# A planned hybrid decoder layer on one core: later assumed landings, dearer ScalarE operations, another table of places in the queues

## The chip, the core and the metric

The kernel runs on one core of a Trainium2 chip. The metric is the device time of one execution in microseconds; the time before is the median of three runs. The five engines are TensorE (PE; PEld is its loading of weights), VectorE (DVE), ScalarE (ACT), GpSimd (POOL) and SyncE (SP). Each takes its instructions from its own queue in the order in which they were issued. SyncE and GpSimd also issue the transfers (DMAs) that bring the weights from the chip's memory.

## What is computed

One layer of a decoder trunk on x of 512 x 1024, in float32. One normed input goes through one combined projection into three groups of heads; a projection merges them; a dense SwiGLU network (width 2816) follows; both halves are residual.

```python
h = rmsnorm(x, norm_mix); mem_h = rmsnorm(mem, norm_mem)
proj = h @ w_in                                  # 1024 -> c_q, c_kv, k_rope, hq, hf, hi, hg, mq
y_mla = mla_group(...)                           # 4 heads, low-rank q and kv, rotary part, causal softmax
y_hg  = hgrn2_group(...)                         # 4 heads, gated linear recurrence in chunks of 64
y_mem = mem_group(mq, mem_h, w_mem_kv, ...)      # 4 heads, softmax over 256 memory tokens
x = x + concat(norm(y_mla), y_hg, norm(y_mem)) @ w_out
h2 = rmsnorm(x, norm_ffn)
x = x + (silu(h2 @ w_gate) * (h2 @ w_up)) @ w_down
```

The kernel reads w_in as `in_we`, `in_wf` and others, x transposed as `in_xT`, w_out as `in_wo`, w_gate, w_up and w_down as `in_wg`, `in_wu` and `in_wd`.

## The kernel before

**Precision.** Each float32 operand of a matmul is split into a rounded high part and the rest. `split` (L527) casts the high part on ScalarE (`A.copy`, or an activation with a scale) and subtracts it on VectorE. A product then takes three matmuls (`mm3`, L557): high by high, high by low, low by high. Tiles `xh`, `xl`, `wh`, `wl`, and `wr` in halves, hold such parts. A weight tile therefore passes through a transfer, a cast and a subtraction before TensorE can use it.

**Stages.** The program starts with the combined projection: tiles of x (`tm`, scaled by the gains in `p`) and of the weights (`p`, `tc`, then `wr`) are split, and the sum of squares of x is formed beside it (`td` <- `tm`). It goes on with the three groups of heads, the merging projection, and the feed-forward network from about 345 us on.

**Feed-forward network.** Its products are made in blocks of columns (512, 512, 384 of one half of the width, each with its partner in the other half). Within a block `seven` forms a two-by-two block product with seven products in place of eight. It loads weight tiles of 128 x 512 (128 x 384 in the last block) through SyncE's queue into the tags `mx`, `y` and at the start `xl`, and forms sums of weight blocks in place: GpSimd issues a transfer that adds a further block to the tile in the chip's on-core memory. This is `more(i, j)`:

```python
G.dma_start(out=e[k], in_=block(k, i, j), accum_op=ALU.add)
```

So a tile such as `mx_1099` is loaded, split and used, added to, split and used, and so on: an addition can be issued once the last split of the old contents has read the tile, and the next split waits for its landing. There are 105 such added transfers, 24 into `mx` from `in_wg`, 24 from `in_wu` and 33 from `in_wd` of 256 KB each, and 24 of 192 KB. `part` splits a tile with class 0 (`rec.first(0)`), that is, ahead of all other work. `prod` multiplies into two accumulator banks, `mm` and `at`.

**What sets the order.** No engine's order is written by hand. Class `Recorder` records every operation with the tiles it reads and writes. `run` (L266) then plans them: it walks through the operations with an assumed time for each, keeps for each engine the time at which it is free, and takes at each step the operation that can start first; among those that can start on the engine when it is free, the one of lowest `prio`, which is its number in the recording, plus 1,000,000 times its class, plus what the table `NUDGE` (L264) adds to it: a triple (a, b, d) adds d to operations a to b. Some operations may run on another engine (`alts`, from `others`): a copy, a square or a scaling on ScalarE or VectorE, say; the planner takes the engine that ends first, with 775 ns added for the move of one from ScalarE. A tile's buffer must have come free before an operation can write it. A transfer is assumed to land a time after its issue (L377 to L381), one transfer after another at 156 bytes per ns for GpSimd's and 320 for SyncE's. The times are `price` and `whole` (L186 and L204) and the table `LAT` between engines. `issue` (L404) then emits all instructions in the order planned; nothing of the planner is left at run time, where engines wait for each other by semaphores. In the profile all instructions carry the line at which `issue` emits them: L421 for groups of small matmuls, L424 for the rest. They are told apart by their tiles.

Names in the order below are tag, a number of the planner's that is the same in both programs, and a last number that is not.

Of the kernel before, what the change touches and what calls it, by code (L numbers as in the profile page):

```python
# [13 lines left out]
AF = mybir.ActivationFunctionType  # L14
# [33 lines left out]
class Recorder:  # L48
# [155 lines left out]
    def whole(self, o, ins, outs, n, m, fast):  # L204
        if o.eng == "scalar":
            fn = o.args[2] if o.name == "activation" else None
            if fn is not None:
                o.table = self.TABLES.get(str(fn).split(".")[-1])
            return (92 if fast else 45) + 0.835 * m + 90 * (fn == AF.Identity) + (190 if "accum_out" in o.kw else 0) + (100 if hasattr(o.kw.get("scale"), "ap") else 0)
        if o.eng == "vector":  # L210
            if o.name == "reciprocal":
                return 70 + 6.6 * m
            if o.name == "tensor_copy":
                return 66 + (0.55 if fast else 1.045) * m
            if o.name == "tensor_scalar":
                return 66 + (0.62 if fast else 1.045) * m + 60 * any(hasattr(a, "ap") for a in o.args[2:])
            if o.name == "memset":
                return 60 + 0.5 * m
            if o.name == "scalar_tensor_tensor":
                return 68 + 1.15 * m + 35 * hasattr(o.args[2], "ap")  # L220
            if o.name == "copy_predicated":
                return 118 + 1.045 * m
            return 68 + 1.045 * m
        if o.name == "memset":
            return 40 + m * 0.8
        if o.name == "tensor_scalar":
            return 244 + 0.84 * m
        return 170 + 2.17 * m
# [32 lines left out]
    IDLE = (1500, 3400)  # L261


    NUDGE = ((2288, 2299, 387), (4374, 4382, -19), (4519, 4568, -844), (1296, 1302, -1004), (4402, 4409, -54), (157, 208, -367), (1352, 1371, -477), (5505, 5507, -189), (3475, 3494, -1244), (3004, 3012, 13), (1981, 1982, 11), (374, 387, 86), (5158, 5164, -409), (4936, 4949, -66), (2039, 2066, 109), (1766, 1791, 700), (5579, 5592, -127), (5092, 5093, 164), (5378, 5383, 4), (4927, 4949, 130), (3745, 3796, -698), (3888, 3900, -443), (2600, 2610, -213), (2695, 2738, 57), (4403, 4409, -124), (3203, 3246, 29), (4683, 4734, 658), (782, 796, 421), (5455, 5461, -180), (1150, 1155, -13), (1118, 1129, -322), (5054, 5083, 300), (1955, 1976, -875), (435, 466, -183), (3034, 3049, 360), (2480, 2485, 125), (1486, 1510, 506), (3927, 3974, 15), (838, 880, 51), (4246, 4299, -11), (4243, 4268, -128), (4968, 4980, 162), (4356, 4372, -422), (2864, 2887, -16), (4823, 4831, -197), (2659, 2715, -5), (3944, 3945, 418), (2504, 2557, 78), (3092, 3101, 181), (265, 314, 7), (1719, 1724, 487), (785, 801, 227), (5531, 5543, 142), (3807, 3827, 371), (2712, 2764, 109), (1167, 1186, -349), (1413, 1457, -103), (2088, 2135, -179), (2654, 2675, 567), (4407, 4430, -251), (4998, 5015, 558), (2506, 2520, 59), (4792, 4801, 623), (3418, 3421, 1704), (4492, 4534, 47), (1999, 2011, 180), (1032, 1053, 351), (2940, 2973, 43), (2342, 2370, -524), (4945, 4949, 65), (283, 341, -78), (3368, 3376, 203), (981, 1004, 166), (5390, 5434, -9), (2863, 2922, 12), (3124, 3131, 58), (5026, 5031, 41), (986, 1036, 31), (5393, 5404, -387), (1584, 1640, -228), (4625, 4645, -63), (5120, 5124, 159), (4517, 4523, -32), (4646, 4660, 136), (3540, 3543, 351), (1664, 1667, -44), (1604, 1616, 232), (4454, 4455, -205), (2319, 2327, -158), (3890, 3932, 286), (4837, 4850, -602), (2173, 2184, 400), (2196, 2213, 100), (3099, 3150, -67), (3010, 3012, -13), (1765, 1782, 46), (1613, 1637, -942), (3968, 4014, -315), (681, 687, 478), (2089, 2118, 151), (4473, 4480, -5), (4342, 4360, -239), (4300, 4329, -247), (4580, 4586, -302), (4623, 4627, -518), (5114, 5133, -411), (1030, 1054, -249), (3123, 3150, -402), (4224, 4258, 339), (528, 532, -414), (1005, 1041, 511), (3895, 3915, 10), (3561, 3603, -80), (3309, 3371, 49), (3754, 3786, -555), (1978, 1990, -17), (722, 754, 255), (4588, 4598, -203), (3993, 4049, -99), (1133, 1146, -551), (3666, 3728, -142), (4921, 4949, -47), (2431, 2433, 243), (1381, 1382, 977), (5605, 5621, -133), (5366, 5377, -640), (1769, 1831, -65), (4434, 4436, 39), (711, 721, -102), (2277, 2312, -350), (4851, 4855, -387), (5404, 5417, -692), (619, 658, -92), (5274, 5289, -151), (3283, 3285, 245), (4700, 4733, -106), (1372, 1391, -127), (3205, 3216, 98), (3835, 3885, -48), (4510, 4513, 144), (5137, 5140, 108), (110, 169, -223), (1668, 1687, -350), (1323, 1342, -428), (1225, 1243, 213), (3020, 3073, -71), (1272, 1300, 293), (2106, 2122, 136), (2236, 2251, 496), (4226, 4287, -111), (4435, 4447, 110), (1237, 1247, -668), (4605, 4618, -147), (3583, 3615, 261), (1206, 1213, 35), (3202, 3209, 61), (4758, 4786, -239), (4462, 4490, 199), (3887, 3915, 15), (4719, 4729, 252), (4733, 4737, 334), (4528, 4580, -30), (2956, 2971, 461), (3693, 3700, -341), (3132, 3151, -7), (5044, 5090, -97), (528, 551, 98), (4222, 4225, -222), (907, 912, 509), (2209, 2240, 451), (4626, 4627, -165), (1908, 1923, -343), (3028, 3053, 287), (1468, 1496, 673), (3599, 3600, 15), (3961, 3963, -457), (5287, 5300, -16), (4511, 4543, -69), (549, 555, 115), (2739, 2743, 61), (234, 295, 19), (5417, 5460, 8), (983, 1021, -500), (2347, 2377, 72), (2923, 2931, -919), (1874, 1889, -470), (3315, 3355, -484), (721, 727, 196), (1444, 1493, 148), (829, 865, 1745), (3054, 3071, 190), (5475, 5483, -404), (5095, 5099, -388), (3004, 3013, 415), (3664, 3670, 70), (3080, 3090, -171), (5127, 5145, -201), (1968, 1997, 371), (1114, 1130, 88), (1485, 1527, 198), (4377, 4381, -462), (141, 164, 263), (3731, 3773, -617), (2059, 2060, 229), (3693, 3698, -518), (1539, 1551, 340), (4957, 5007, -149), (2211, 2235, -51), (860, 875, -93), (2154, 2174, 223), (5474, 5475, -141), (2610, 2650, -713), (4428, 4454, -53), (4834, 4842, -60), (1340, 1393, -154), (3696, 3734, -656), (4488, 4511, -408), (2676, 2716, -630), (1052, 1088, 267), (3650, 3651, 83), (311, 342, -148), (4295, 4298, 594), (4901, 4920, 34), (2118, 2144, 5), (2126, 2131, 378), (1978, 1993, 11), (4816, 4823, -117), (1725, 1764, -585), (4522, 4526, 113), (2880, 2896, 116), (3914, 3941, 8), (4556, 4557, 12), (1640, 1641, 1213), (1723, 1773, 218), (2024, 2062, -69), (4399, 4450, 29), (2857, 2870, -13), (113, 148, 169), (3422, 3458, -61), (2075, 2117, 34), (3605, 3614, -179), (3892, 3894, 292), (2940, 2944, -54), (5053, 5070, -584), (3245, 3260, 210), (964, 974, -167), (5514, 5545, -299), (4180, 4181, 243), (5423, 5437, 5), (4459, 4463, 133), (4212, 4228, -356), (780, 812, -89), (1883, 1888, 312), (3692, 3698, 150), (2011, 2039, 83), (5028, 5051, -44), (5572, 5597, 275), (4962, 4969, 122), (4902, 4909, 38), (4597, 4644, 338), (1627, 1660, 172), (369, 372, 683), (5261, 5274, -2958), (1781, 1796, -643), (5037, 5087, -219), (5249, 5266, -610), (5101, 5127, -73), (3067, 3080, 161), (1800, 1821, 296), (2144, 2156, 109), (1941, 1951, -634), (4197, 4232, 470), (3166, 3232, -158), (1549, 1560, 558), (277, 290, 124), (5172, 5175, 30), (3437, 3461, 45), (430, 440, -159), (5468, 5474, -26), (582, 588, 807), (3112, 3130, -644))  # L264

    def run(self):  # L266
        ops = self.ops
# [21 lines left out]
        table, dma, done, out, port, cold = None, 0.0, 0, [], 0.0, 0.0  # L289
        busy = {e: 0.0 for e in engs}  # L290
        begun, count = -1e9, self.AHEAD
        while done < len(ops):
# [79 lines left out]
            end = t + cost  # L372
# [4 lines left out]
            if o.dma:  # L377
                ap = o.kw["out"]
                nb = self._free(ap) * ap.ap[0][1] * 4
                dma = max(dma, t + 1100) + nb / (156.0 if o.eng == "gpsimd" else 320.0)  # L380
                end = dma + (2600 if o.eng == "gpsimd" else 1700)  # L381
            for k in o.new:
                tag = self.tiles[k][0]
                slots[tag].remove(min(slots[tag]))
# [1270 lines left out]
```

## Time and profile before

| | us |
|---|---|
| three runs | 693.21, 690.7, 689.88; median 690.7 |
| the profiled execution, its own time | 686.31 |
| its span in the profile | 684.5 |
| TensorE busy (matmuls) | 675.5 |
| VectorE busy | 589.6 |
| ScalarE busy | 397.5 |
| GpSimd busy | 98.7 |
| moved by transfers | 95.16 MB, mean 139 GB/s |

The profile is of one execution. A matmul's record includes the time in which it overlaps the one behind it, so that busy time on TensorE leaves out a part of each short stop. The number in brackets at the end of a row of the timeline is how long the engine was idle before the instruction, and whose end released it. In a row of busy time by stage the numbers are start and end, length, and for each engine its busy time and the count of instructions, then TensorE's granted clock, the share of time in which the core's 16 DMA engines were busy, and the GB/s that they moved.

### The profile page before, as it was taken

To read this page: it belongs to the slowest core of one execution; us is meant where nothing else is said; L and a number is where in the kernel's file an instruction comes from. 1 tells how busy PE (TensorE), PEld (TensorE's weight loads), DVE (VectorE), ACT (ScalarE), POOL (GpSimd) and SP (SyncE) were. 2 spreads that over 40 slices of the span, in tenths; PEclk is the share of its full clock that TensorE was granted. 3 is DMA by queue.
4 is the path that set the end of the run, shared out by engine and by line. 5 is a ranking of instruction groups with operands and counts; after the bars stand their busy time and mean duration, and the time that the engine had idled before them with its cause. 6 is when DMAs were issued, how large, how long until landed. Compare 5 with 4: busy or idle time off the path is not lost.

```text
span 684.5 us, 12877 instructions
## 1 busy us (share of the span) xinstructions
PE 675.5 (99%) x4684; PEld 560.8 (82%) x4684; DVE 589.6 (86%) x1313; ACT 397.5 (58%) x784; POOL 98.7 (14%) x132
## 2 busy tenths in 40 slices
PE   9999999999999999999999999999999999999997
PEld 5889978888888788888878788878878898889985
DVE  7879889889888989886779889778986988997996
ACT  7674346566667585665868546355643555553652
POOL 1000000000000000000122232223323133323330
PEclk9999999999999999999999999999999999999999
DMA  8522321032233143214387796887887778879754
GB/s 295 179 58 87 98 67 36 32 126 74 92 109 128 61 139 125 78 60 161 103 182 156 195 203 157 177 221 168 173 214 138 165 179 197 179 168 191 155 84 150
DMA packets 47871, 95.16 MB, mean 139 GB/s; under 512 B 5440, under 2 KB 13504, under 8 KB 47808
## 3 DMA queue, kind: packets, MB, share of 16 engines
q1 hardware_dynamic: 32256, 67.85, 30.2%
q0 software_dynamic: 15120, 25.96, 24.2%
q8 instruction: 37, 0.61, 0.4%
q10 hardware_dynamic: 432, 0.53, 0.2%
q14 instruction: 26, 0.21, 0.1%
HBM read 92.22 MB, written 2.10 MB: 138 GB/s over the span
## 4 chain that ended last, share of the span: by engine, by line
PE 73%; issue 13%; DMA 6%; POOL 4%; DVE 2%; ACT 1%; POOLq 0%; ACTq 0%; DVEq 0%
PE mm L424 45%; PE at L424 20%; PE tr L424 5%; POOL mx L424 4%; DMA mx<-in_wg 2%; DMA mx<-in_wu 2%; PE at L421 1%; DMA tc<-in_we 1%; DMA xl<-in_wg 1%; PE tr L421 1%; ACT wh L424 1%; DVE hd L424 0%; DVE tm L424 0%; DVE wl L424 0%; ACT hd L424 0%
## 5 line engine op out<-in xcount | busy, mean ns | idle before, releaser
L424 ACT CAST wh<-wr 128x512 fp32r<-128x512 f32 (+2 forms) x73 | 42.9, 597 | 46.6 <-PE mm L424 34.3
L424 ACT CAST wr<-mx 128x512 fp32r<-128x512 f32 (+1 forms) x77 | 45.6, 598 | 39.9 <-PE at L424 18.9
L424 DVE TENSOR_TENSOR wr<-mx,wr 128x512 fp32r<-128x512 f32 (+1 forms) x94 | 60.8, 658 | 5.7 <-ACT wr L424 5.0
L424 ACT CAST wh<-mx 128x512 fp32r<-128x512 f32 (+1 forms) x71 | 41.9, 598 | 38.0 <-PE at L424 25.8
L424 PE MATMUL mm<-xh,wh 128*128 128x512 f32 x152 | 59.8, 396 | 0.4 <-ACT wh L424 0.4
L424 PE MATMUL mm<-xl,wh 128*128 128x512 f32 x152 | 59.7, 395 | 0.0
L424 PE MATMUL mm<-xh,wl 128*128 128x512 f32 x152 | 59.5, 397 | 0.0
L424 DVE TENSOR_TENSOR wl<-wr,wh 128x512 fp32r<-128x512 f32 (+2 forms) x88 | 57.1, 659 | 2.8 <-PE mm L424 1.4
L424 DVE TENSOR_TENSOR wl<-mx,wh 128x512 fp32r<-128x512 f32 (+1 forms) x81 | 52.4, 659 | 4.7 <-PE at L424 1.9
L424 POOL DMA_DIRECT2D mx<-in_wg x36 | 31.4, 921 | 127.5 <-DVE wl L424 57.6
L424 PE MATMUL mm<-wh,xh 128*128 128x512 f32 (+2 forms) x136 | 47.3, 372 | 0.4 <-ACT wh L424 0.2
L424 PE MATMUL mm<-wh,hd 128*128 128x512 f32 (+2 forms) x140 | 44.4, 366 | 0.8 <-ACT wh L424 0.7
L424 POOL DMA_DIRECT2D mx<-in_wu x36 | 31.6, 917 | 86.4 <-DVE wl L424 42.6
L424 PE MATMUL mm<-wh,mx 128*128 128x512 f32 x128 | 44.0, 403 | 0.0
L424 ACT CAST wh<-y 128x512 fp32r<-128x512 f32 (+1 forms) x50 | 29.1, 594 | 23.7 <-PE at L424 16.6
L424 DVE TENSOR_TENSOR wl<-y,wh 128x512 fp32r<-128x512 f32 (+1 forms) x52 | 33.1, 652 | 7.7 <-PE at L424 2.7
L424 POOL DMA_DIRECT2D mx<-in_wd x33 | 28.7, 924 | 74.9 <-DVE wl L424 42.6
L424 POOL MEMSET pb<- 128x128 f32 x15 | 2.8, 204 | 234.5 <-PE at L424 209.1
L424 PE MATMUL mm<-wl,xh 128*128 128x512 f32 (+2 forms) x92 | 33.2, 361 | 0.6 <-DVE wl L424 0.6
L424 PEld LDWEIGHTS mm<-xh,wh 128*128 128x128 f32 x152 | 28.5, 188 | 6.2 <-ACT wh L424 0.5
L424 PEld LDWEIGHTS mm<-xh,wl 128*128 128x128 f32 x152 | 28.7, 189 | 5.5 <-DVE wl L424 0.2
L424 PEld LDWEIGHTS mm<-xl,wh 128*128 128x128 f32 x152 | 28.6, 188 | 5.6
(459 smaller groups left out, 1941.4 us busy)
## 6 DMA issues: line engine op xcount, KB each, us to landing
wr<-in_wf SPq DMA_DIRECT2D x19, 512.0 KB, 4.3
mx<-in_wd POOLq DMA_DIRECT2D x33, 256.0 KB, 5.0
wr<-in_wo SPq DMA_DIRECT2D x12, 512.0 KB, 3.8
mx<-in_wg POOLq DMA_DIRECT2D x24, 256.0 KB, 5.2
mx<-in_wu POOLq DMA_DIRECT2D x24, 256.0 KB, 5.0
mx<-in_wd SPq DMA_DIRECT2D x22, 256.0 KB, 4.1
y<-in_wd SPq DMA_DIRECT2D x22, 256.0 KB, 4.6
wr<-in_wt SPq DMA_DIRECT2D x8, 512.0 KB, 3.6
```

What stands on the lines that cost most here:

```text
L421: r = self.nc.tensor.matmul(get(a), lhsT=get(b), rhs=get(c), start=first, stop=last, skip_group_check=True)
L424: r = getattr(getattr(self.nc, o.eng), o.name)(*[get(a) for a in o.args], **{k: get(a) for k, a in o.kw.items()})
```

## The change

Three places of the planner change; no operation that is recorded does. ScalarE's assumed time of an operation rises by 8 ns where its inputs lie in on-core SBUF memory and by 11 ns otherwise. The assumed landing of each transfer is 0.8 us later on both queues. The table `NUDGE` is replaced: it had 281 triples and has 142, with other ranges and amounts.

```diff
--- before.py
+++ after.py
@@ -206,7 +206,7 @@
             fn = o.args[2] if o.name == "activation" else None
             if fn is not None:
                 o.table = self.TABLES.get(str(fn).split(".")[-1])
-            return (92 if fast else 45) + 0.835 * m + 90 * (fn == AF.Identity) + (190 if "accum_out" in o.kw else 0) + (100 if hasattr(o.kw.get("scale"), "ap") else 0)
+            return (100 if fast else 56) + 0.835 * m + 90 * (fn == AF.Identity) + (190 if "accum_out" in o.kw else 0) + (100 if hasattr(o.kw.get("scale"), "ap") else 0)
         if o.eng == "vector":
             if o.name == "reciprocal":
                 return 70 + 6.6 * m
@@ -261,7 +261,7 @@
     IDLE = (1500, 3400)
 
 
-    NUDGE = ((2288, 2299, 387), (4374, 4382, -19), (4519, 4568, -844), (1296, 1302, -1004), (4402, 4409, -54),
...
+    NUDGE = ((3247, 3249, 155), (4519, 4569, -1372), (295, 318, -135), (5018, 5033, 50), (640, 641, 177),
...
 
     def run(self):
         ops = self.ops
@@ -378,7 +378,7 @@
                 ap = o.kw["out"]
                 nb = self._free(ap) * ap.ap[0][1] * 4
                 dma = max(dma, t + 1100) + nb / (156.0 if o.eng == "gpsimd" else 320.0)
-                end = dma + (2600 if o.eng == "gpsimd" else 1700)
+                end = dma + (3400 if o.eng == "gpsimd" else 2500)
             for k in o.new:
                 tag = self.tiles[k][0]
                 slots[tag].remove(min(slots[tag]))
```

The instructions are the same in number and kind on TensorE and SyncE; a few operations change their engine: VectorE gets seven scalings of 128x128 more and ScalarE eight activations of that size fewer, GpSimd two more scalings, ScalarE six of VectorE's casts of 128x384, and the loads of function tables on ScalarE go from 12 to 10.

**The head.** On TensorE the first matmuls of the projection, into the accumulators `at_59` and `at_61`, from the second one after the warm-up on. `xh_17`, `xh_21`, `xh_25` are the high parts of the first three tiles of x, `wh_15`, `wh_19`, `wh_23` those of the first weight tiles. Before:

```order
L424 MATMUL at_59_1857<-xh_17_1845,wh_15_1837 128x512
L424 MATMUL at_61_1855<-xl_18_1853,wh_15_1837 128x512
L424 MATMUL at_61_1855<-xh_17_1845,wl_16_1843 128x512
L424 MATMUL at_61_1855<-xh_21_1860,wh_19_1849 128x512
L424 MATMUL at_59_1857<-xl_18_1853,wh_15_1837 128x512
L424 MATMUL at_59_1857<-xh_17_1845,wl_16_1843 128x512
L424 MATMUL at_59_1857<-xh_21_1860,wh_19_1849 128x512
L424 MATMUL at_61_1855<-xl_22_1869,wh_19_1849 128x512
L424 MATMUL at_61_1855<-xh_21_1860,wl_20_1862 128x512
L424 MATMUL at_59_1857<-xl_22_1869,wh_19_1849 128x512
L424 MATMUL at_59_1857<-xh_21_1860,wl_20_1862 128x512
L424 MATMUL at_61_1855<-xh_25_1881,wh_23_1875 128x512
```

and now:

```order
L424 MATMUL at_61_1861<-xh_17_1848,wh_15_1841 128x512
L424 MATMUL at_59_1855<-xl_18_1853,wh_15_1841 128x512
L424 MATMUL at_59_1855<-xh_17_1848,wl_16_1845 128x512
L424 MATMUL at_59_1855<-xh_21_1859,wh_19_1851 128x512
L424 MATMUL at_59_1855<-xl_22_1872,wh_19_1851 128x512
L424 MATMUL at_59_1855<-xh_21_1859,wl_20_1865 128x512
L424 MATMUL at_61_1861<-xl_18_1853,wh_15_1841 128x512
L424 MATMUL at_59_1855<-xh_25_1884,wh_23_1876 128x512
L424 MATMUL at_61_1861<-xh_17_1848,wl_16_1845 128x512
```

The accumulator of the other half now runs behind, and the first matmul with `xh_25` is the 9th, where it was the 13th. On ScalarE, the casts and squares that feed them (the first row is the high part of the second tile of x), before:

```order
L424 ACTIVATE xh_21_1860<-tm_5_1814,p_2_1801 128x512
L424 ACTIVATE td_41_1866<-tm_3_1805 128x512
L424 CAST wh_23_1875<-tc_6_1817 128x512
L424 ACTIVATE xh_25_1881<-tm_7_1819,p_2_1801 128x512
L424 ACTIVATE xh_27_1891<-tm_8_1823,p_2_1801 128x512
```

and now:

```order
L424 ACTIVATE xh_21_1859<-tm_5_1814,p_2_1801 128x512
L424 ACTIVATE td_41_1870<-tm_3_1805 128x512
L424 CAST wh_23_1876<-tc_6_1817 128x512
L424 ACTIVATE td_42_1879<-tm_5_1814 128x512
L424 ACTIVATE xh_25_1884<-tm_7_1819,p_2_1801 128x512
L424 ACTIVATE xh_27_1891<-tm_8_1823,p_2_1801 128x512
```

The square of `tm_5`, which VectorE did, now stands on ScalarE between `wh_23` and `xh_25`.

**A product of the first block.** On VectorE, from the split of `mx_1099` whose reading lets the second addition into that tile start (`wl_1135`), up to the split of the sum (`wl_1148`). `td` and the like are the sums of the seven products. Before:

```order
L424 TENSOR_TENSOR wl_1135_7337<-mx_1099_6824,wh_1134_7295 128x512
L424 TENSOR_TENSOR wl_1137_7344<-mx_1100_6868,wh_1136_7334 128x512
L424 TENSOR_TENSOR wl_1142_7351<-y_1112_7100,wh_1141_7341 128x512
L424 TENSOR_TENSOR td_1091_7329<-mm_1124_7227,td_1091_7329 128x512
L424 TENSOR_TENSOR wl_1144_7371<-y_1113_7116,wh_1143_7348 128x512
L424 TENSOR_TENSOR wl_1146_7381<-y_1114_7121,wh_1145_7374 128x512
L424 TENSOR_TENSOR wr_1140_7386<-y_1111_7056,wr_1140_7386 128x512
L424 CAST wh_1147_7402<-mx_1099_6824 128x512
L424 TENSOR_TENSOR wl_1148_7408<-mx_1099_6824,wh_1147_7402 128x512
```

and now:

```order
L424 TENSOR_TENSOR wl_1135_7310<-mx_1099_6841,wh_1134_7292 128x512
L424 CAST wr_1139_7319<-mx_1102_6900 128x512
L424 TENSOR_TENSOR wl_1137_7323<-mx_1100_6847,wh_1136_7314 128x512
L424 TENSOR_TENSOR wr_1139_7319<-mx_1102_6900,wr_1139_7319 128x512
L424 TENSOR_TENSOR wl_1142_7337<-y_1112_7063,wh_1141_7326 128x512
L424 TENSOR_TENSOR wr_1138_7334<-mx_1101_6858,wr_1138_7334 128x512
L424 TENSOR_TENSOR wl_1144_7350<-y_1113_7075,wh_1143_7341 128x512
L424 CAST wr_1140_7368<-y_1111_7055 128x512
L424 TENSOR_TENSOR wr_1140_7368<-y_1111_7055,wr_1140_7368 128x512
L424 COPY td_1091_7383<-mm_1115_7297 128x512
L424 TENSOR_TENSOR wl_1146_7388<-y_1114_7093,wh_1145_7353 128x512
L424 TENSOR_TENSOR td_1091_7383<-mm_1124_7223,td_1091_7383 128x512
```

The next row is the split `wl_1148`. The parts `wr_1139` and `wr_1138` are now formed between the two, and the cast `wh_1147` has gone to ScalarE.

**The last block of gate and up, and the first of down.** On ScalarE, from `wr_1418`, a part of the last gate and up block, on; `wh_1445`, `wh_1447` and `wh_1449` are the first of the down projection. Before:

```order
L424 CAST wr_1418_8667<-mx_1357_8020 128x384
L424 ACTIVATE tc_1350_8658<-tc_1350_8658,r2_996 128x384
L424 CAST wh_1419_8685<-mx_1358_8031 128x384
L424 CAST wh_1445_8694<-mx_1423_8326 128x512
L424 ACTIVATE tm_1353_8520<-tm_1353_8520,r2_996 128x384
L424 CAST wh_1447_8708<-mx_1424_8372 128x512
L424 CAST wh_1449_8716<-mx_1425_8415 128x512
```

and now:

```order
L424 CAST wr_1418_8678<-mx_1357_8050 128x384
L424 CAST wh_1445_8692<-mx_1423_8378 128x512
L424 CAST wh_1447_8698<-mx_1424_8391 128x512
L424 CAST wh_1449_8705<-mx_1425_8421 128x512
L424 ACTIVATE tm_1353_8531<-tm_1353_8531,r2_996 128x384
L424 CAST wh_1419_8718<-mx_1358_8059 128x384
```

The cast `wh_1419`, whose tile `mx_1358` is added to by GpSimd's transfer, moves behind the three. On SyncE's queue, the loads of the down projection, before:

```order
L424 DMA y_1435_8580<-in_wd 128x512
L424 DMA mx_1427_8632<-in_wd 128x512
L424 DMA y_1436_8649<-in_wd 128x512
L424 DMA y_1437_8665<-in_wd 128x512
L424 DMA y_1438_8672<-in_wd 128x512
L424 DMA mx_1428_8683<-in_wd 128x512
```

and now:

```order
L424 DMA y_1435_8607<-in_wd 128x512
L424 DMA y_1436_8624<-in_wd 128x512
L424 DMA y_1437_8630<-in_wd 128x512
L424 DMA y_1438_8652<-in_wd 128x512
L424 DMA mx_1427_8662<-in_wd 128x512
L424 DMA mx_1428_8676<-in_wd 128x512
```

The loads of `y_1436` to `y_1438` are issued ahead of that of `mx_1427`.

More of the change, by code (lines that the diff above doesn't have):

```diff
@@ new lines @@
+    NUDGE = ((3247, 3249, 155), (4519, 4569, -1372), (295, 318, -135), (5018, 5033, 50), (640, 641, 177), (3381, 3442, -139), (2895, 2918, 153), (5423, 5424, 172), (3587, 3615, 261), (974, 1004, 166), (5075, 5110, 35), (2910, 2917, -36), (5128, 5153, -187), (389, 428, 174), (4877, 4884, -76), (3986, 4047, -53), (2947, 3007, -50), (4331, 4335, 131), (4510, 4517, 223), (5158, 5160, -30), (4353, 4387, -36), (4374, 4386, -273), (731, 761, 65), (719, 754, 255), (829, 869, 2881), (4355, 4394, -55), (3926, 3927, 12), (4034, 4036, 154), (3711, 3770, 122), (883, 894, -55), (4051, 4052, -560), (388, 395, -95), (4947, 4949, 104), (510, 544, 266), (3163, 3166, 111), (5054, 5083, 546), (4682, 4744, 17), (4802, 4803, -8), (5092, 5093, 63), (5037, 5087, -195), (4170, 4198, -172), (5383, 5390, 57), (44, 56, -271), (1916, 1929, 48), (2975, 3002, 78), (5419, 5465, 23), (3004, 3013, 415), (967, 986, 393), (1167, 1186, -391), (3696, 3734, -656), (1968, 1987, 84), (5495, 5510, -44), (4346, 4395, 88), (5533, 5548, -719), (5474, 5488, 4), (714, 720, -70), (2018, 2022, -98), (4329, 4331, 96), (5141, 5142, 7), (970, 983, -537), (2949, 2972, 76), (1492, 1531, 40), (5048, 5088, -82), (5493, 5503, 195), (375, 380, 157), (5134, 5162, 62), (3793, 3825, -97), (3628, 3646, -103), (3044, 3059, 528), (4790, 4822, -70), (804, 808, 23), (1899, 1909, -158), (1005, 1044, 511), (1272, 1300, 802), (4287, 4308, 693), (4967, 4968, 277), (4597, 4601, 40), (4030, 4052, 24), (3440, 3483, 134), (5028, 5047, -57), (5261, 5274, -3656), (1781, 1796, -535), (3692, 3731, 109), (5158, 5161, -13), (3693, 3709, -191), (5515, 5545, -299), (5032, 5045, 66), (4931, 4994, 27), (4062, 4079, -4), (964, 974, -233), (983, 1021, -895), (4410, 4436, -251), (2665, 2706, 618), (5053, 5070, -584), (4705, 4708, 721), (3674, 3722, 79), (965, 974, -279), (4135, 4136, -10), (4443, 4502, 69), (4197, 4232, 470), (395, 447, -51), (4458, 4515, -104), (4719, 4736, 212), (4771, 4823, -497), (2209, 2240, 451), (4138, 4139, 447), (3745, 3796, -698), (3948, 4004, -75), (289, 301, 389), (4137, 4153, 164), (582, 588, 807), (4997, 5049, 35), (4479, 4502, -42), (3350, 3388, 18), (3303, 3304, 88), (5096, 5102, -20), (2619, 2641, 29), (4569, 4621, -35), (2132, 2164, -132), (3590, 3631, -26), (2878, 2901, 152), (3815, 3827, 1366), (5414, 5422, 132), (4973, 4976, 19), (358, 406, 736), (2944, 2972, 27), (5151, 5156, 490), (5117, 5123, 251), (4370, 4381, 41), (681, 693, 401), (2318, 2346, -33), (2816, 2817, 265), (2031, 2043, -234), (721, 727, 179), (4216, 4222, -628), (5114, 5133, -367), (5150, 5158, -212), (5578, 5603, 97), (1190, 1191, 13), (4483, 4524, -350), (754, 782, -83), (4459, 4515, 334))
```

1 line of the change is left out of this document (removed).

## The prediction

> **What bounds the kernel now.** I read the page's head and busy line first, then busy time by stage, then the chain of waits, and last the timeline of TensorE at each place where it stops. The page says:
>
> ```profile
> span 684.5 us, 12877 instructions
> PE 675.5 (99%) x4684; PEld 560.8 (82%) x4684; DVE 589.6 (86%) x1313; ACT 397.5 (58%) x784; POOL 98.7 (14%) x132
> PEclk9999999999999999999999999999999999999999
> ```
>
> TensorE is busy for 675.5 of 684.5 us at full granted clock, so all its idle time is 9.0 us. Its matmuls run at a fixed spacing: the chain holds twelve in a row without a wait, and these two transfers:
>
> ```profile
> 438.75 6.73 DMA mx<-in_wg
> ...
> 505.16 6.79 DMA mx<-in_wu
> ...
> 603.39 2.72 PE mm L424 x12
> ```
>
> 2.72/12 = 0.227 us for a matmul of 512 columns, three quarters of that (0.17) for 384. The orders of the two programs hold the same matmuls, so what can change is TensorE's stops. By stage (length, then busy time of PE, PEld, DVE, ACT and POOL, PE clock, share of the DMA engines, GB/s):
>
> ```profile
> 0.00:20.00 20.00, 18.46 (x67) 11.72 (x68) 15.06 (x26) 14.58 (x26) 2.39 (x9) 1.00 0.73 253
> ...
> 60.00:120.00 60.00, 59.43 (x1037) 51.51 (x1036) 53.40 (x155) 28.42 (x67) 0.00 (x0) 1.00 0.23 75
> 120.00:180.00 60.00, 59.95 (x621) 50.42 (x620) 54.96 (x157) 37.24 (x75) 1.48 (x8) 1.00 0.24 80
> 180.00:240.00 60.00, 59.68 (x304) 49.16 (x303) 52.30 (x138) 38.01 (x79) 0.77 (x4) 1.00 0.30 97
> 240.00:300.00 60.00, 59.90 (x472) 49.82 (x471) 52.25 (x149) 39.46 (x97) 2.40 (x6) 1.00 0.29 98
> 300.00:360.00 60.00, 59.85 (x343) 47.57 (x343) 45.73 (x103) 42.18 (x93) 6.20 (x7) 1.00 0.54 145
> 360.00:440.00 80.00, 79.93 (x365) 64.65 (x365) 72.63 (x128) 45.11 (x79) 21.35 (x25) 1.00 0.79 179
> 440.00:480.00 40.00, 39.26 (x171) 31.48 (x170) 31.18 (x53) 22.66 (x38) 9.69 (x12) 1.00 0.85 192
> 480.00:520.00 40.00, 39.31 (x171) 31.45 (x171) 35.58 (x60) 20.29 (x35) 10.89 (x14) 1.00 0.88 190
> ...
> 560.00:600.00 40.00, 39.19 (x200) 34.56 (x200) 36.20 (x66) 23.67 (x45) 11.97 (x14) 1.00 0.87 199
> ...
> 670.00:684.50 14.50, 10.51 (x45) 7.92 (x44) 8.69 (x17) 3.01 (x6) 0.00 (x0) 0.99 0.39 134
> ```
>
> Subtract PE from length. The first 20 us lose 1.54 and the last 14.5 lose 3.99, mostly start and drain. The attention and projection stages (60 to 360) lose 0.57 + 0.05 + 0.32 + 0.10 + 0.15 = 1.19. The feed-forward stages lose 0.07 + 0.74 + 0.69 + 0.81 = 2.31, all but 0.07 of it in those where the DMA engines are 0.85 to 0.88 busy. A matmul's record (about 0.39) is longer than its spacing (0.227), so busy time hides some 0.17 of each stop: a stop is therefore measured from start to start.
>
> **FFN landings: minus 3.0 us.** TensorE at the four worst places:
>
> ```profile
> 444.54 0.84 PE L424 MATMUL mm<-wr,v 128*128 128x512 f32 x3
> 446.05 0.50 PE L424 MATMUL mm<-wh,v 128*128 128x512 f32 x1 [0.67 <-DVE wh L424]
> ...
> 511.64 0.39 PE L424 MATMUL at<-wh,hd 128*128 128x512 f32 x1
> 512.72 0.50 PE L424 MATMUL mm<-wh,hd 128*128 128x512 f32 x1 [0.69 <-ACT wh L424]
> ...
> 574.32 0.34 PE L424 MATMUL at<-wh,pth 128*128 128x384 f32 x1
> 574.87 0.50 PE L424 MATMUL mm<-wh,xh 128*128 128x512 f32 x1 [0.21 <-ACT wh L424]
> 575.20 0.40 PE L424 MATMUL at<-wh,xh 128*128 128x512 f32 x1
> ...
> 575.96 0.33 PE L424 MATMUL mm<-wr,pth 128*128 128x384 f32 x1
> 576.89 0.50 PE L424 MATMUL mm<-wl,xh 128*128 128x512 f32 x1 [0.60 <-DVE wl L424]
> ```
>
> At 446.05 three matmuls from 444.54 should have been followed at 445.22: 0.83 late. At 512.72: 1.08 - 0.23 = 0.85. At 574.87: 0.55 - 0.17 = 0.38. At 576.89: 0.93 - 0.17 = 0.76. After a stop the second matmul starts 0.33 behind the first (574.87 to 575.20), not 0.227, so each costs 0.11 more. Sum: 0.83 + 0.85 + 0.38 + 0.76 + 4 x 0.11 = 3.26. I take 3.0, since a later stop of some tenths is likely to be left at one of them.
>
> The cause is a landing each time. The first two are the chain's transfers: added in place by a GpSimd DMA issued at 438.75 and 505.16, landed 6.73 and 6.79 later, where the medians are
>
> ```profile
> mx<-in_wg POOLq DMA_DIRECT2D x24, 256.0 KB, 5.2
> mx<-in_wu POOLq DMA_DIRECT2D x24, 256.0 KB, 5.0
> ```
>
> The other two are behind a waiting instruction:
>
> ```profile
> 573.78 1.03 ACT L424 CAST wh<-mx 128x384 fp32r<-128x384 f32 x2 [0.68 <-DMA mx<-in_wg]
> ...
> 575.54 0.69 DVE L424 TENSOR_TENSOR y<-y,y 128x512 f32<-128x512 f32 x1 [0.66 <-DMA y<-in_wd]
> ```
>
> ScalarE stood 0.68 for wh_1419's input with wh_1445 queued behind; VectorE stood 0.66 for y_1436 with wl_1446 queued behind.
>
> The planner assumes for 262,144 bytes on GpSimd's queue, if no other transfer is ahead, 1100 + 262144/156 + 2600 ns = 5.38 us: the median with a little room, but 1.4 less than the two late ones. Now it is 6.18. What that buys is counted in the order. Between the matmul that lets the second addition into mx_1099 start and the first that needs the sum stand 29 matmuls before (29 x 0.227 = 6.6 us, less than the 6.73 plus cast and split), and 37 now (8.4). For mx_1265 it is 30 (6.8) against 40 (9.1). ScalarE now has wh_1445, wh_1447 and wh_1449 ahead of wh_1419, and SyncE issues y_1436 ahead of mx_1427, which waits for a VectorE read. So all four stops go. Over all 105 added transfers, 13 leads were shorter than 32 matmuls (7.3 us), now 6; the shortest few (2 and 14 matmuls) stay. If those take the place of what went, the gain is 0; if the later small stops go too, 3.5.
>
> [...]
>
> **The program's head: plus 1.1 us.** Matmuls 13 and 14, 15, and 17 of the first projection, and ScalarE ahead of them:
>
> ```profile
> 9.36 0.73 PE L424 MATMUL at<-xh,wh 128*128 128x512 f32 x2
> 10.15 0.50 PE L424 MATMUL at<-xl,wh 128*128 128x512 f32 x1
> ...
> 10.72 0.40 PE L424 MATMUL at<-xh,wh 128*128 128x512 f32 x1
> ```
>
> ```profile
> 7.12 0.62 ACT L424 ACTIVATE td<-tm 128x512 f32<-128x512 f32 x1
> 8.06 0.63 ACT L424 CAST wh<-tc 128x512 fp32r<-128x512 f32 x1 [0.33 <-DMA tc<-in_we]
> 8.60 1.33 ACT L424 ACTIVATE xh<-tm,p 128x512 fp32r<-128x512 f32 x2
> ```
>
> The square td_42 moves from VectorE to ScalarE, between wh_23 (8.06) and xh_25 (8.60). ScalarE starts its next operation 0.54 after one of this size (8.06 to 8.60), so xh_25 starts near 9.13 in place of 8.60. Its first matmul came 0.76 after that start (9.36) and so comes at 9.89. It is also the 9th matmul in place of the 13th, so the four that used to fill the time stand behind it. The 17th then starts at 9.89 + 0.33 + 7 x 0.227 = 11.8 against 10.72: 1.1 later. The first ten loads are the same, so no transfer gives this back; if the later squares leave ScalarE freer, 0.8, and 1.3 if the next splits slip too.
>
> **The middle: 0.** In the stages from 60 to 360 the order changes in many rows, seven scalings of 128x128 move from ScalarE to VectorE, and two table loads go:
>
> ```profile
> L424 DVE TENSOR_SCALAR tm<-tm,rkn 128x128 f32<-128x128 f32 x4 | 1.0, 284 | 0.0
> ```
>
> ```profile
> L424 ACT ACT_TABLE_LOAD x12 | 15.4, 1283 | 2.3 <-issue 2.1
> ```
>
> 7 x 0.284 = 2.0 us more for VectorE, which is at most 55 of 60 busy there; 2 x 1.283 = 2.6 less for ScalarE, at most 42 of 60. Both lie beside matmuls, and TensorE's whole loss there is 1.19. A dense VectorE could turn the 2.0 into a wait, and the loads could have been what it waited for: minus 2 to plus 2, taken as 0, since the idle rows are nearest to it.
>
> **The tail: plus 0.1.** One of the last two accumulators is finished nine matmuls ahead of the other and the last operand comes some 0.2 later; the closing addition and the output transfer are the same.
>
> **The sum.** The profiled execution took 686.3 (span 684.5 and 1.8 around it). 686.3 - 3.0 + 1.1 + 0.0 + 0.1 = 684.5, so minus 1.8. The timed runs, 689.88 to 693.21, have their median 690.7, which is 4.4 above the profiled one: executions differ by more than the stops seen here. With one program at one clock, transfers that land later than in this trace are the candidate. If they are, longer leads take part of the 4.4; a quarter, 1.1, is my choice between none and all. 690.7 - 1.8 - 1.1 = 687.8.
>
> **The rivals.**
> *The excess goes too.* If all 4.4 us are late landings and the leads now cover them: 690.7 - 1.8 - 4.4 = 684.5. For it: at 0.85 to 0.88 busy engines, landings have a long tail (6.7 to 6.8 against 5.0 to 5.2). Against: some leads stay short, and the excess may lie in the start.
> *The leads buy nothing.* If landings are late because transfers queue on shared engines, issuing earlier only queues earlier, and the stops come back elsewhere. Only the head's 1.1 is left: 691.8. For it: the stops stand where the engines are busiest (0.85, 0.88, 0.87). Against: what the leads gain is eight to ten matmuls, 1.8 to 2.3 us, more than any of the stops.
> *Slower.* Earlier issue bunches the loads; at 440 to 520 the engines have an eighth left. If the old stops stay and three more transfers land as late as the first two (0.85 + 0.11 each), 3 x 0.96 = 2.9 is added beside the head: 690.7 + 1.1 + 2.9 = 694.7. It decides from a median landing above 6 us on GpSimd's queue. Against: bytes and bank reads are the same, and the queues' waits for reads bind them as before.
>
> **How the numbers follow.** Forecast 42%, excess gone 25%, leads worthless 18%, slower 15%. About 0.5%, 3.45 us, is what a measurement of this kernel can tell from no change: faster is below 687.2, slower above 694.2. The forecast's own range is 685.3 to 690.3 (middle plus or minus 2, quarter or half a us of the leads); it splits into 16% faster and 26% same. The second case gives 23 and 2, the third 15 same and 3 slower, the fourth 2 same and 13 slower. Together 39, 45 and 16%. The range runs from 683.0, below the second case by its unknown middle, to 694.0, which leaves out most of the slow case.
>
> **What would show it.** Right: no stop above 0.5 us at the four places, GpSimd's medians still 5.0 to 5.2, a TensorE idle sum in the feed-forward stages below 1 us, and the first xh-by-wh matmul of the third pair at about 9.9. Wrong: new stops above 0.5 behind other landings; medians above 6 us; more than 2 us of idle time from 60 to 360 with VectorE as releaser; or a profiled time near 684.5 with timed runs that keep their 4.4 or more.

## The result and the profile after

The changed kernel takes 684.23 us (median of 8 runs, 682.09 to 685.23) beside 688.45 for the kernel before (8 runs, 687.01 to 693.21): a ratio of 0.9925 over all runs, with a 95% interval of 0.9899 to 0.9951 (the two medians alone give 0.9939). A second measurement, told with the experiments, has 0.9944. By the medians of the two it is faster by 4.2 and 3.7 us. The forecast was a fall of 2.9 us, to 687.8.

The profiled execution took 682.81, 3.5 less than that of before:

```profile
span 681.0 us, 12877 instructions
PE 672.5 (99%) x4684; PEld 562.4 (83%) x4684; DVE 588.5 (86%) x1312; ACT 393.8 (58%) x781; POOL 100.3 (15%) x134
```

The same stages as before (start and end, length, busy time of PE, PEld, DVE, ACT and POOL, TensorE's granted clock, share of the DMA engines, GB/s):

```profile
0.00:20.00 20.00, 16.66 (x60) 10.50 (x61) 14.26 (x26) 14.58 (x26) 2.38 (x9) 1.00 0.74 253
...
60.00:120.00 60.00, 59.50 (x1037) 51.25 (x1037) 51.87 (x150) 28.18 (x65) 0.00 (x0) 1.00 0.24 75
120.00:180.00 60.00, 59.91 (x617) 50.39 (x616) 55.56 (x164) 34.70 (x70) 1.52 (x8) 1.00 0.25 80
...
440.00:480.00 40.00, 40.00 (x177) 32.34 (x176) 32.95 (x55) 23.08 (x38) 9.58 (x12) 1.00 0.88 198
480.00:520.00 40.00, 40.00 (x177) 32.69 (x176) 34.34 (x58) 20.77 (x36) 11.33 (x13) 1.00 0.84 181
...
560.00:600.00 40.00, 40.00 (x201) 35.75 (x200) 38.40 (x70) 22.92 (x44) 13.08 (x15) 1.00 0.88 191
```

TensorE is now busy all the time in the stages where it stood 0.74, 0.69 and 0.81 us, with the DMA engines as busy as before. The first 20 us lose 3.34 in place of 1.54. What went is seen in the waits for landings between 340 and 670 us. Each row gives engine, tile, the transfer waited for, total us, times and the longest. Before, ScalarE and VectorE:

```profile
ACT wh L424 <- DMA mx<-in_wu: 6.5, 5, 2.5
ACT wr L424 <- DMA mx<-in_wg: 4.8, 1, 4.8
ACT wh L424 <- DMA mx<-in_wg: 1.8, 3, 0.7
ACT wr L424 <- DMA mx<-in_wd: 1.6, 2, 1.3
ACT wr L424 <- DMA mx<-in_wu: 0.3, 1, 0.3
...
DVE y L424 <- DMA y<-in_wd: 1.4, 2, 0.8
DVE wh L424 <- DMA mx<-in_wg: 1.1, 1, 1.1
```

With four small rows of VectorE's more that is 20 us in 20 waits. In the changed kernel VectorE has none, and ScalarE these:

```profile
ACT wh L424 <- DMA mx<-in_wd: 3.2, 2, 2.5
ACT wh L424 <- DMA mx<-in_wu: 1.8, 2, 1.3
```

The transfers themselves land no sooner. GpSimd's added ones take 5.9 us at the median from in_wg, where they took 5.2:

```profile
mx<-in_wd POOLq DMA_DIRECT2D x33, 256.0 KB, 4.9
mx<-in_wg POOLq DMA_DIRECT2D x24, 256.0 KB, 5.9
mx<-in_wu POOLq DMA_DIRECT2D x24, 256.0 KB, 5.2
```

Counted in the traces, 10 of the 105 added transfers took over 6.5 us before, and 19 and 17 in the two profiles of the changed kernel. So the order gives the landings more time, and does not make them earlier.

For the account below, the time that TensorE loses in a stretch is summed from start to start: the distance between two matmuls, less the usual spacing of that shape (0.227 us for 512 columns). Unlike idle time this sees short stops in full. In us:

| stretch | before | changed | difference |
|---|---|---|---|
| first 20 us | 2.08 | 3.66 | +1.58 |
| 20 to 340 | 15.30 | 15.96 | +0.66 |
| from 340 | 8.44 | 2.74 | -5.70 |
| together | 25.82 | 22.36 | -3.46 |

### The profile page after: what moved, and what is told of

The parts are those of the page before. It is cut to its first block, busy times and chain, and to the rows that moved or that the text cites. A ratio compares the mean times of both kernels' runs of the same rounds, so it can differ in the third digit from the quotient of the medians.

```text
span 681.0 us, 12877 instructions
## 1 busy us (share of the span) xinstructions
PE 672.5 (99%) x4684; PEld 562.4 (83%) x4684; DVE 588.5 (86%) x1312; ACT 393.8 (58%) x781; POOL 100.3 (15%) x134
## 4 chain that ended last, share of the span: by engine, by line
PE 58%; DVE 4%; issue 0%; ACT 0%; DVEq 0%; ACTq 0%
PE mm L424 31%; PE at L424 24%; PE tr L424 3%; DVE tm L424 1%; DVE wl L424 1%; DVE xh L424 1%; DVE wr L424 0%; DVE tc L424 0%; DVE v L424 0%; DVE xl L424 0%; PE tr L421 0%; ACT wh L424 0%; DVE hd L424 0%; DVE pb L424 0%; DVE mvq L424 0%
## 5 line engine op out<-in xcount | busy, mean ns | idle before, releaser
L424 ACT CAST wh<-wr 128x512 fp32r<-128x512 f32 (+2 forms) x76 | 44.4, 595 | 43.5 <-PE mm L424 25.8
L424 ACT CAST wh<-mx 128x512 fp32r<-128x512 f32 (+1 forms) x75 | 43.7, 597 | 30.9 <-PE at L424 22.4
L424 PE MATMUL at<-wh,xh 128*128 128x512 f32 x88 | 31.9, 393 | 0.0
```

Of the source, the lines that this page charges most:

```text
L424: r = getattr(getattr(self.nc, o.eng), o.name)(*[get(a) for a in o.args], **{k: get(a) for k, a in o.kw.items()})
```

## The experiments

Seven of the twelve kernels run a written-out order: the planner's loop is replaced by two lists, and all that comes after it is unchanged.

```diff
     def run(self):
-        ops = self.ops
-        for a, b, d in self.NUDGE:
...
+        names = {"t": "tensor", "v": "vector", "s": "scalar", "g": "gpsimd", "y": "sync"}
+        out = []
+        for n, e in zip(ORDER, WHERE):
+            o = self.ops[n]
+            o.eng = names[e]
+            o.name, o.args, o.kw = o.alts[o.eng][:3]
+            out.append(o)
+        return out
```

ORDER holds the numbers of the operations and WHERE the engine of each, taken from the plan of before, from the changed plan, or from one up to a planned time and the other behind it; in two kernels some places are then moved by hand. Times are medians; the kernel before ran at 687.0 to 687.1 beside all of them.

### The changed kernel once more

Without an edit, beside 20 runs of the kernel before. 

> The changed kernel once more, beside the runs of before that the experiments share. Theory (its gain is the 3.5 us between the two traces, feed-forward network minus head and middle): 687.04 - 3.5 = 683.5, a ratio of 0.995. Rival (the first ratio of 0.9925 holds): 681.9.

Measured: 683.38 us (9 runs, 682.77 to 686.06) against 687.10, a ratio of 0.9944 (0.9921 to 0.9967): what the two traces give. The profiled execution of this measurement is one of the longer ones, 685.93; the last section tells why.

### Where the gain lies: the two plans joined

**The head of before, then the changed order** (joined at 20 us). 

> The first 20 us of the planned order are those of before, all that follows is in the changed order. Theory (the changed order of ScalarE and TensorE at the head costs 1.1 us): 1.1 below the changed kernel, 683.1, and TensorE loses 2.1 to 2.5 us in its first 20 us where the changed kernel lost 3.7. Rival (the first loads only landed later in that one execution, and the order at the head is harmless): 684.2, the same as the changed kernel, and a loss of 3.2 or more.

Measured: 682.95 us (0.9940, 0.9926 to 0.9954). The row of its first 20 us:

```profile
0.00:20.00 20.00, 18.32 (x64) 11.66 (x65) 14.50 (x25) 14.13 (x25) 2.39 (x9) 1.00 0.75 253
```

TensorE idles 1.68 there, near the 1.54 of before. Summed from start to start it loses 2.7, a little more than the 2.1 to 2.5 expected, and less than the rival's 3.2. So the order at the head does cost time. The median of 682.95 is only 0.4 below the 683.38 of the changed kernel's second measurement, and 1.0 below the median of all its 17 runs, 683.98.

**The order of before up to 340 us, then the changed one.** 

> The planned order of before up to 340 us, then that of the changed kernel. Theory (the whole gain lies in the feed-forward network, where the trace of before loses 8.4 us to stops and that of the changed kernel 2.7): 688.45 - 5.7 = 682.8, faster than the changed kernel by some 1.4. Rival (only the four stops of the prediction go, 3.3 us, and the rest is a difference between executions): 685.2. Second rival (the gain lies ahead of the feed-forward network or in both): above 687.

Measured: 683.59 (0.9952, 0.9939 to 0.9966), where 682.8 was expected of the theory. From 360 us on it is the changed kernel's picture, and one wait between 340 and 360 us, at the seam, takes 2.2 us:

```profile
360.00:660.00 300.00, 300.00 (x1440) 256.01 (x1439) 266.47 (x473) 168.18 (x306) 82.10 (x95) 1.00 0.81 179
```

```profile
PE mm L424 <- DVE hd L424: 2.2, 1, 2.2
```

That wait belongs to the joining: neither of the two kernels has it. The expected 682.8 was counted from 688.45; from the 687.10 beside this kernel the gain is 3.5, and with the seam's 2.2 it is the theory's 5.7. The time alone would suit the first rival's gain of 3.3 as well; what decides is that TensorE's stops between 360 and 660 us are gone.

**The changed order up to 340 us, then that of before.** 

> The planned order of the changed kernel up to 340 us, then that of before. Theory: 688.45 + 1.1 (head) + 0.7 (middle) = 690.2, with the late landings and TensorE's stops of before back in the feed-forward network. Rival (the early part brings some of the gain): 687 or less.

Measured: 692.26 (1.0077, 1.0063 to 1.0091). Here too the seam costs some 2.1 us, and the stops of the feed-forward network are back, behind the same kind of landing:

```profile
360.00:660.00 300.00, 297.07 (x1416) 250.08 (x1415) 263.39 (x468) 161.67 (x294) 82.17 (x95) 1.00 0.81 177
```

```profile
ACT wh L424 <- DMA mx<-in_wu: 7.5, 6, 1.8
ACT wr L424 <- DMA mx<-in_wg: 6.5, 2, 5.7
...
DVE y L424 <- DMA y<-in_wd: 4.1, 3, 2.0
```

So the gain is in the order from 340 us on, whatever runs ahead of it; which of the many changes of place there carry it, no run takes apart. In the four profiled executions with the changed order there, TensorE loses 2.6 to 3.4 us from 360 us on, and in the two with the old one 7.3 and 7.9.

### One stop taken away by hand

The prediction put the stops at 574.87 and 576.89 down to instructions queued behind one that waits. Two kernels move just those. First: ScalarE's wh_1419 three casts later, VectorE's split of it and three additions behind wl_1450. 

> The kernel before with five instructions moved: ScalarE's cast wh_1419 behind wh_1449, VectorE's split wl_1420 and the three additions of y_1436 to y_1438 behind wl_1450. Nothing lands earlier. Theory (the two stops near 575 us are instructions queued behind one that waits for a landing): both go, 0.38 + 0.76 + 2 x 0.11 = 1.4, so 687.1. Rival (TensorE needs what lands, wherever the cast stands): the stops come back within 10 us at the matmuls with wh_1419, and the time stays at 688.4.

Measured: 691.86 (1.0066, 1.0051 to 1.0082), slower by 4.8, which neither side expected. Both stops went, and a worse one came at 585 us. The chain of waits there, and ScalarE:

```profile
576.13 0.56 DVE wl L424
576.69 0.02 issue
576.71 6.97 DMA mx<-in_wd
...
583.78 0.63 ACT wh L424
```

```profile
583.78 0.62 ACT L424 CAST wh<-mx 128x512 fp32r<-128x512 f32 x1 [4.50 <-DMA mx<-in_wd]
584.30 0.61 ACT L424 CAST wr<-mx 128x512 fp32r<-128x512 f32 x1
```

The split that was moved back was the last reader of a buffer. The load into that buffer is issued at 576.71 and lands at 583.68, and ScalarE stands 4.50 us for it, with the cast that TensorE needs queued behind. In the trace of before the same load is issued at 574.91 and lands at 578.69. So it starts 1.8 later, but also takes 6.97 where it took 3.78. GpSimd's queue, ahead of it:

```profile
574.62 0.86 POOL L424 DMA_DIRECT2D mx<-in_wd  x1 [5.94 <-DVE wl L424]
575.90 1.75 POOL L424 DMA_DIRECT2D mx<-in_wd  x2 [0.42 <-DVE wl L424]
```

VectorE's earlier splits let three additions go out in the 2.1 us ahead of the load; in the trace of before the next addition goes out 2.2 us behind it. The second kernel delays no reader that a load waits for. 

> The kernel before with the cast wh_1419 only one place later on ScalarE, behind wh_1445, and on VectorE the split wl_1420 behind wl_1446 and the additions of y_1436 to y_1438 behind wl_1448. The reads that set transfers free come no later than before. Theory (a stop is what is queued behind an instruction that waits for a landing, and a move costs nothing as long as it delays no read that a load waits for): both stops near 575 us go and no new one of over 0.5 us comes within 20 us, 687.04 - 1.4 = 685.6. Rival (moving the queue places only moves the stops): 687 or more.

Measured: 688.68 (1.0022, 1.0002 to 1.0042): no gain. The rival has the time right. The two stops went again, but between 570 and 590 us TensorE loses 1.51, where the kernel before loses 1.52. What ScalarE waits for now is the same load as in the first kernel. GpSimd's addition and the cast of the loaded tile, in the kernel before:

```profile
577.13 0.86 POOL L424 DMA_DIRECT2D mx<-in_wd  x1 [8.34 <-DMA mx<-in_wd]
...
580.34 0.61 ACT L424 CAST wh<-mx 128x512 fp32r<-128x512 f32 x1
```

and in this one, with the load from its chain of waits:

```profile
575.82 0.86 POOL L424 DMA_DIRECT2D mx<-in_wd  x1 [5.95 <-DVE wl L424]
...
576.02 5.78 DMA mx<-in_wd
...
581.90 0.62 ACT L424 CAST wh<-mx 128x512 fp32r<-128x512 f32 x1 [1.66 <-DMA mx<-in_wd]
```

Ahead of the moved instructions this execution runs 1.08 late (VectorE's split of an earlier part starts at 573.44, and at 572.36 before). Less that, the load is issued at 574.94, where it was before (574.91), but lands 2.0 later: it takes 5.78 in place of 3.78. ScalarE was free for the cast at 580.24. Had the load taken as long as before, it would have landed at 579.80, and ScalarE would not have waited.

One addition now goes out ahead of the load, and none did before. In the three traces the load takes 3.78, 5.78 and 6.97 us with none, one and three additions issued in the 2.1 us ahead of it. That the additions, which VectorE's earlier splits release, slow the load is the author's reading and not shown: no run varies the additions alone, and the 22 loads from in_wd into `mx` on SyncE's queue take 2.52 to 7.65 us within the one trace of before. Shown is that the median of 12 runs has no gain.

One other stop of the prediction is missing in both kernels, though their order is that of before up to there: the one at 512.72. Its transfer took 6.79 us in the trace of before, and 5.66 and 5.30 in these. It was a late landing of that one execution. The one at 446.05 comes again, behind transfers of 6.18 and 6.66.

### The parts of the diff, each alone

First the table of before with the changed times of transfers and of ScalarE; the first of the two stands here:

```diff
-                end = dma + (2600 if o.eng == "gpsimd" else 1700)
+                end = dma + (3400 if o.eng == "gpsimd" else 2500)
```

> The changed assumed landings and ScalarE times with the table of before. Counted in the order, 16 of the 105 added transfers then have a lead under 32 matmuls, where before has 13 and the changed kernel 6. Theory (a table fits the times that it was chosen with, and the leads decide): slower than before by 1 to 5 us, with at least as many stops behind landings in the feed-forward network as before. Rival (the later assumed landings alone pull loads forward): 684 to 686.

Measured: 696.04 (1.0133, 1.0102 to 1.0165), slower by 9.0, which is more than the theory's 5, and mostly not where the theory had it. From 360 to 660 us TensorE loses 0.9 more than in the kernel before; the first 20 us lose 2.8 more, with a granted clock of 0.91 in place of 1.00, and the end behind 660 us 5.3 more. From 340 to 670 us ScalarE and VectorE wait for landings 7.8 us in 7 waits (20 in 20 before), and TensorE's longest wait, 2.1 us, names VectorE's `tm`. So the waits for landings became fewer, though 16 leads are short, and the run does not bear out that the leads decide. The rival's 684 to 686 falls too.

Then the new table with the times of before. 

> The new table with the assumed landings and ScalarE times of before: 11 leads under 32 matmuls. Theory: about the time of before or up to 4 us slower, with stops behind landings. Rival (the table alone carries the gain): 683 to 685.

Measured: 723.22 (1.0524, 1.0490 to 1.0557), slower by 36, which neither side had in mind. Most of it is lost from 260 to 300 us, where TensorE waits up to 2.9 us at a time for VectorE's softmax tiles, and its granted clock falls to 0.83 and 0.60:

```profile
260.00:280.00 20.00, 12.14 (x53) 9.51 (x53) 15.16 (x50) 8.09 (x22) 0.99 (x3) 0.83 0.28 92
280.00:300.00 20.00, 13.96 (x198) 11.37 (x199) 16.08 (x47) 6.62 (x12) 0.00 (x0) 0.60 0.16 54
```

The kernel before is busy for 19.96 and 20.00 us there. In both crossed kernels the table costs more than no table would with the same times, as the next two runs show.

The changed times without any table (`NUDGE = ()`). 

> No table at all, with the changed times: 4 leads under 32 matmuls. Theory (the leads decide what the feed-forward network loses): from 360 us on TensorE loses 3 us or less, as in the changed kernel (2.6), while the stages ahead of it lose more than in either kernel, so that the whole is slower than before. Rival (leads don't decide): 5 us or more lost from 360 us on.

Measured: 688.78 (1.0036, 1.0018 to 1.0055). TensorE hardly stops from 360 to 660 us, and loses in the stages ahead and at the end:

```profile
20.00:340.00 320.00, 315.20 (x2997) 263.73 (x2997) 271.10 (x755) 189.59 (x391) 8.75 (x22) 0.99 0.30 97
...
360.00:660.00 300.00, 299.90 (x1442) 257.36 (x1441) 252.86 (x441) 183.65 (x335) 83.17 (x96) 1.00 0.80 178
```

Its loss from 360 us on is 4.4, above the 3 expected, but 3.1 of that comes after 660 us, in the drain. With 4 short leads the network has few stops; the stops ahead of it and at the end are of another kind.

The times of before without a table. 

> No table, with the times of before: 3 leads under 32 matmuls. Theory: within 2 us of the kernel without a table and with the changed times, and 3 us or less lost from 360 us on. Rival (the assumed landings by themselves decide the stops): 2 us or more slower than that one, with the difference in the feed-forward network.

Measured: 691.30 (1.0067, 1.0046 to 1.0089). Without a table the changed times alone bring 2.5 us, a little more than the 2 that the theory allowed, and both kernels have few stops in the network (a loss of 2.6 from 360 to 660 us here, 1.3 there). From 360 us on this one loses 5.7 with the drain, above the 3 expected. About half of the 2.5 lies in the network, so the rival is half right. Whether the later landings or the dearer ScalarE brings it, no run separates. The old table brought 4.3 on top of its times, and the new one 5.4 on top of its own.

Over the six plans, TensorE loses 1 to 3 us from 360 to 660 us where 3, 4 or 6 leads are short, and 7 to 11 where 11, 13 or 16 are. So the count sorts them in two groups, but not within a group (11 leads lose 11, 16 lose 8), and in the two crossed kernels the profile's longest waits of TensorE there name other tiles than weights. That short leads make the stops is read from the traces of the order of before; no run changes the leads alone.

### The added transfers, later

To see how much room the leads have, GpSimd does two small operations ahead of each added transfer, on the tile that the transfer adds to:

```diff
+            if o.dma and o.eng == "gpsimd":
+                x = get(o.kw["out"])[:, 0:1]
+                for _ in range(2):
+                    self.tc.keep_in_program_order(self.nc.gpsimd.tensor_scalar(x, x, 1.0, None, ALU.mult))
```

In the kernel before: 

> The kernel before with two multiplications by 1.0 of one column on GpSimd ahead of each of the 105 added transfers, which write the tile that is added to, so that each of these transfers is issued some 0.5 to 0.8 us later; the result is the same. Theory (before has no room in its leads: 13 under 32 matmuls): 2 to 5 us slower than before, with more stops behind landings from 360 us on. Rival (landings have room, the stops have other causes): less than 1 us slower.

In the changed kernel: 

> The same delay in the changed kernel, with 6 leads under 32 matmuls. Theory (its longer leads take the delay): 0 to 1.5 us slower than the changed kernel, and less than half of what the same delay costs the kernel before. Rival (both lose alike): the same added time as in the kernel before.

Measured: 725.70 (1.0539) and 705.99 (1.0245), so the delay costs 38.6 us in the kernel before and 22.6 in the changed one. Both sizes were far too low: an operation takes 0.495 us, and with the wait of 0.3 behind the two each transfer is some 1.3 us later, not 0.5 to 0.8; where several follow one another on GpSimd's queue this adds up. A part of both costs is TensorE's granted clock, which is 0.97 and 0.98 on average from 360 to 660 us, and 1.00 in the two kernels without the delay.

```profile
L427 POOL TENSOR_SCALAR mx<-mx 128x1 f32<-128x1 f32 x210 | 103.9, 495 | 206.3 <-DVE wl L428 109.5 <-DMA xl<-in_wg 42.3 <-DVE wr L428 40.9
```

The sign stands: the changed order bears the same delay at 0.59 of the cost (theory: under half). The theory's 0 to 1.5 us for the changed kernel is missed by far, and the rival's equal cost does not hold either. That both suffer so much shows that neither order has room for a delay of this size at every transfer; the room of the changed one is larger, and small.

## Why the prediction was right, and where its terms were off

The direction, the place and the stated range held. The size did not come from the sum: its terms give -1.8, and the two traces differ by 3.5, since the feed-forward term fell short by 2.7 and the head and the middle took back 1.1 more than forecast. The forecast of -2.9 is nearer to the measured 3.7 and 4.2 only by its last 1.1, which had no ground; that is luck. The time of 687.8 is 3.6 above the measured 684.23, which lies outside the forecast's own 685.3 to 690.3, and within 683.0 to 694.0 because that range is wide.

**FFN landings, -3.0: right mechanism, too small.** All four stops are gone, as forecast, and in the first profile TensorE waits for nothing that the profile names from 340 to 670 us. The term measured -5.7. It counted four stops (3.26) and took 0.26 off for one that would be left. One of the four was of that one execution, as the kernels moved by hand show; other executions with this order have other stops, so what the order loses is more than the largest stops of one trace. The smaller ones count too. TensorE in the kernel before:

```profile
351.64 0.39 PE L424 MATMUL at<-wr,hd 128*128 128x512 f32 x1
352.16 0.50 PE L424 MATMUL mm<-wh,hd 128*128 128x512 f32 x1
...
380.90 0.61 PE L424 MATMUL at<-wr,pth 128*128 128x512 f32 x2
381.59 0.50 PE L424 MATMUL at<-wl,hd 128*128 128x512 f32 x1
381.93 0.39 PE L424 MATMUL at<-wh,hd 128*128 128x512 f32 x1
```

They show no idle time, since the matmul's record covers it, but 352.16 is 0.29 late and 381.59 is 0.23 late, with 0.11 behind each. The stretch from 340 to 360 us alone lost 1.1 and now loses 0.1. The bound of 3.5 was too narrow for the same reason.

The picture of single stops was wrong in one respect. The sum treated each as a price that goes when the instruction ahead is moved; in the two kernels moved by hand, stops went and another came at a later landing, where a load was issued later or took longer. What the changed plan moves is the whole sequence of reads and loads.

**The head, +1.1: right mechanism, too small, and a second price.** ScalarE and TensorE in the changed kernel:

```profile
8.48 0.62 ACT L424 CAST wh<-tc 128x512 fp32r<-128x512 f32 x1 [0.66 <-DMA tc<-in_we]
9.00 0.63 ACT L424 ACTIVATE td<-tm 128x512 f32<-128x512 f32 x1
9.53 1.32 ACT L424 ACTIVATE xh<-tm,p 128x512 fp32r<-128x512 f32 x2
```

```profile
8.70 0.39 PE L424 MATMUL at<-xl,wh 128*128 128x512 f32 x1
10.29 0.50 PE L424 MATMUL at<-xh,wh 128*128 128x512 f32 x1 [1.20 <-ACT xh L424]
```

The square stands where it was put, and the first matmul with xh_25 comes at 10.29, 0.40 after the 9.89 forecast. The transfer for wh_23 accounts for that: it lands at 8.45, and landed at 8.04 before (in the kernel with the head of before it lands at 8.64, so this is scatter). Idle time in the first 20 us is 2.5 to 3.7 us in the four profiled executions with the changed head and 1.1 to 2.2 in the six with the old one, means of 3.2 and 1.7: 1.5 where 1.1 was forecast, and above its bound of 1.3. The second price is the clock, below.

**The middle, 0: a loss of 0.7,** inside the bounds of 2 either way. No run here takes it apart.

**From the profile to the median, -1.1: no ground.** The excess of 4.4 us came from three runs. In 20 later runs the kernel before has a median of 687.10, 0.8 above its profiled execution. The rival that gives the whole excess back (684.5) has nearly the right time, but the later runs show no such excess to give back, and the traces put the gain into the feed-forward term. The other rivals fall: leads were worth their time, and the landings that the slow rival feared (5.9 and 6.0 in two profiles in place of 5.2 at in_wg) are there, at the edge of its 6 us, and covered. The prediction's sign that the medians stay at 5.0 to 5.2 did not hold.

## What to carry to other kernels

A stop of the busiest engine in one trace is a symptom: before counting it as a gain, see whether a second execution has it, look for the next landing that could take its place, and ask which read sets that transfer free and which other transfers a move would send ahead of it. Where a planner's numbers and a table of corrections were chosen together, as here, changing one of them alone cost 9 and 36 us. Where landings scatter (the added transfers take 3.50 to 8.07 us in the one trace of before), the order that leaves them more time than their median lost less here, but such an order should be looked at where the program starts, since there nothing covers it.

## What the runs showed of the hardware

With the changed head TensorE's granted clock is lower in some executions. Stretches of 4 us of the changed kernel's second profile:

```profile
4.00:8.00 4.00, 2.86 (x9) 1.04 (x8) 2.35 (x4) 2.58 (x5) 0.41 (x1) 1.00 0.92 278
8.00:12.00 4.00, 2.20 (x7) 1.49 (x8) 2.55 (x5) 3.20 (x6) 0.64 (x2) 0.87 1.03 378
12.00:16.00 4.00, 4.00 (x14) 3.14 (x14) 4.00 (x8) 4.00 (x8) 0.00 (x0) 0.70 0.98 343
```

and two of them in the first:

```profile
8.00:12.00 4.00, 2.67 (x10) 1.91 (x11) 2.95 (x6) 3.52 (x7) 0.92 (x2) 1.00 1.02 362
12.00:16.00 4.00, 4.00 (x19) 3.19 (x18) 4.00 (x7) 3.91 (x7) 0.00 (x0) 1.00 1.01 383
```

The stop before xh_25 is 1.80 us in the second profile, with a granted clock of 0.87 from 8 to 12 us and 0.70 from 12 to 16: 14 matmuls in the latter stretch where the kernel before has 20. 0.13 x 4 + 0.30 x 4 = 1.7 us. In the first profile the stop is 1.20 us, and the clock is 1.00 in both stretches. Over the first 20 us the clock is 0.91 in three of the 14 profiled executions (the changed kernel's second, the kernel with the old feed-forward order, and the table of before with the changed times) and 1.00 in the other eleven; of the four with the changed head two have 0.91, of the six with the old one none.

Of the 17 runs of the changed kernel, 9 have a mean clock of 0.998 or less, with a median of 685.1, and 8 have 0.999 or more, with 683.3. All 11 runs of the two joined kernels with the old head have 0.999 or more. No run varied the head's stop alone, so what lowers the clock there is not shown.
